# Second layer: mixer and both gates token-major, sums of weights from a column of ones, result transposed, norm factor behind the products

## Chip, cores and metric

The kernel runs on one core of a Trainium2 chip. The core has five engines that run side by side, each through its own list of instructions in a fixed order: TensorE (PE, matrix products; PEld is its loading of weights), VectorE (DVE), ScalarE (ACT), GpSimd (POOL) and SyncE (SP, which issues nearly all transfers here). They wait for each other by semaphores. The metric is the device time of one execution in microseconds, lower is better.

## What is computed

A trunk of two layers on 256 tokens of width 2048, in float32. The first layer (HGRN2 and RG-LRU) is not touched. The second is an mLSTM with two gates, then an output projection, a gated per-layer embedding and the final norm. Cut to the part that matters:

```python
hn = rmsnorm(h, o_norm[j])
u = hn @ o_w_in[j]                      # q,k (2048), v, og, z (2048 each), 2 x 8 gates
qk = jax.nn.silu(causal_conv(qk, c_conv_w[j], c_conv_b[j]))
li = ig + c_b_i[j]
lf = jax.nn.log_sigmoid(fg + c_b_f[j])
# mlstm, 8 heads of 128 (q, k) and 256 (v):
sc = jnp.einsum('bhtd,bhsd->bhts', qc, kc) * wts
num = g_inter * (qc @ c_st) + jnp.einsum('bhts,bhse->bhte', sc, vc)
den = g_inter * (qc @ n_st) + jnp.sum(sc, axis=-1)
hout = num / jnp.maximum(jnp.abs(den), jnp.exp(-m_t))[..., None]
# behind it:
yc = head_rmsnorm(hout, c_norm[j]) * jax.nn.sigmoid(og) * jax.nn.silu(z)
h = h + yc @ o_w_out[j]
pl = rmsnorm(p[i] @ ple_w[i], ple_norm[i])
h = h + jax.nn.sigmoid(h @ ple_gate_w[i]) * pl
```

The kernel computes the mLSTM over all 256 tokens at once, without the chunks.

## The kernel before, in words

**Precision.** Each large product is made of three: a float32 operand is split into a high and a low part (`whi`, `wlo` of the weights, both halves of `ahl` for activations), and high x high, high x low and low x high are summed. `load_weights` (L112) brings 128x2048 weights as two halves `raw`, ACT casts the high part (L123) and DVE subtracts (L124). There are five buffers for `raw`, four each for `whi` and `wlo`.

**Two forms of projection.** Feature-major (`block`, L147, through `project`, L182): 128 output features on the partitions, 256 tokens in the columns. 16 products of 512 columns (L154, high weights on both parts of the activations), then 16 of 256 columns (L160, low weights on the high part); `merge` (L177) adds the two halves of the PSUM bank by ACT (L179) and DVE (L180). Token-major (`project_tok`, L189): 128 tokens on the partitions, 512 features in the columns, two banks for the two halves of the tokens; the weights come in four quarters (`kq`), and each quarter has 12 products for each half (L204 to L206). The pool `pm` has three PSUM banks for both.

**Side work.** What is not a projection runs in generators, the lanes ("mix", "norm", "pl"). `pump` (L75) takes each lane one step further, in the middle of each block or quarter, so that its PE instructions lie between a block's products; `drain` runs a lane to its end. From this the framework makes one list per engine ahead of time, by priority, where a tile waits for a free buffer of its tag. The casts of weights have a raised priority.

**The second layer.** `finish_norm` (L471) makes the norm factors of the tokens (`norm["rt"]` with tokens on partitions, `norm["rs"]` with tokens in columns) and the normed activations `act` by `normed` (L300). `acth` is the same without the factor, only with the gain. v is projected token-major from `acth`, and the factor is applied as its result leaves PSUM (L781). The 16 gate columns (L802), q and k (`qk_proj`, L759), `oog` (eight pairs, L935) and `oz` (eight pairs, `gate_split`, L318) are feature-major products on `act`. The 12 buffers of the tag `ahl` hold `acth`, `act`, the embedding's input and the results `y` of the z gate.

**The mixer.** `gate_stats` (L813) makes the decays, their running maximum and `enm`, the Exp that bounds the denominator. `mix(j)` (L852) takes two heads in four steps: the maxima spread over the partitions and the weights' Exp; scores (L874, L875) and weighting; then, into feature-major banks, the sums of weights (L887, L888) and the value products (L892, L893), whose squares are summed by the next call (`head_sums`, L845). `mix_norm` (L903) turns denominators and sums of squares into one factor per head and token, spreads it by PE (L919) and multiplies `nums`. Then come the tanh gates, the splits of `y`, the embedding product `ple` (L339) and `finish_layer` (L382), whose first block reads all eight pairs of `y`.

## Time and profile before

| | |
|---|---|
| median of 3 runs | 1126.47 us (1126.02 to 1127.44) |
| the profiled execution | 1128.03 us |
| its span | 1126.3 us |
| mean granted clock of TensorE | 0.993 |
| share of PE in the chain that ended last | 90% |
| L154, L160: share of that chain | 48%, 25% |
| HBM read, written | 195.17 MB, 2.10 MB |

A profile is one execution. Busy time of an engine is the sum of stretches in which it had an instruction; times are in us from the start of the span unless marked ns. In a list of groups a row reads: line, engine, operation, output<-inputs, shapes and count, then busy time and mean ns of one, then the idle time of the engine before them and what ended it. In a list in order of time a row reads: start, length, engine, line, operation, count, and in brackets the idle time before it. In the chain the length is only the part that the next step waited for. In a table of stages each engine has its busy time and, in parentheses, the number of instructions; PEclk is the granted clock of TensorE. A plain float32 product is recorded as two matrix instructions.

### The profile page before, as it was taken

The page shows a single profiled execution, that of the slowest core. Times are in us where ns is not written, and L with a number is a line of the kernel's source. Part 1 is how long each engine was busy: PE and PEld are TensorE (multiplying, and loading weights), DVE is VectorE, ACT ScalarE, POOL GpSimd, SP SyncE. Part 2 cuts the span into 40 slices and gives each one's busy share as a digit, 9 for nine tenths or more (in the row PEclk, how much of TensorE's full clock was granted, in tenths as well). Part 3 has the DMA queues.
Part 4 walks back from the last instruction along what each step waited for, and adds up shares of the span by engine and source line. Part 5 has one row for each costly group of instructions (what it writes and reads, how often), then busy time and mean ns, then how long its engine had stood idle before and what let it go on. Part 6 is the DMA issues. An engine that isn't in the chain of part 4 may idle for free.

```text
span 1126.3 us, 16657 instructions
## 1 busy us (share of the span) xinstructions
PE 1102.8 (98%) x6344; PEld 958.6 (85%) x6344; DVE 806.6 (72%) x1192; ACT 593.2 (53%) x814; POOL 106.4 (9%) x78
## 2 busy tenths in 40 slices
PE   7999999999999999999999999999999989999996
PEld 6778898888888888888888888888888888888886
DVE  6998776798867656787745876659566568856774
ACT  6575435666645435555545655544455464435553
POOL 2144000000000000111000011110000013500110
PEclk9999999999999999999999999999999989999998
DMA  8655545443566555565555544444565555555542
GB/s 315 205 181 187 167 138 166 149 148 132 170 204 201 192 187 187 187 190 187 190 188 174 183 139 139 150 148 159 192 201 187 188 169 163 192 187 188 189 149 75
DMA packets 55377, 198.36 MB, mean 176 GB/s; under 512 B 6145, under 2 KB 6401, under 8 KB 55297
## 3 DMA queue, kind: packets, MB, share of 16 engines
q1 hardware_dynamic: 54720, 195.20, 52.4%
q0 software_dynamic: 576, 2.10, 0.6%
q8 instruction: 50, 0.82, 0.3%
q14 instruction: 31, 0.25, 0.1%
HBM read 195.17 MB, written 2.10 MB: 175 GB/s over the span
## 4 chain that ended last, share of the span: by engine, by line
PE 90%; DVE 2%; ACT 1%; issue 0%; POOL 0%; ACTq 0%; DVEq 0%; POOLq 0%
PE mm L154 48%; PE mm L160 25%; PE mm L204 2%; PE mm L206 2%; PE mm L205 2%; PE mx L589 2%; PE mx L892 1%; DVE wlo L124 1%; PE mx L687 1%; PE mm L171 1%; PE mm L143 0%; PE mm L144 0%; PE tr L959 0%; PE mm L145 0%; PE mx L277 0%
## 5 line engine op out<-in xcount | busy, mean ns | idle before, releaser
L124 DVE TENSOR_TENSOR wlo<-raw,whi 128x1024 fp32r<-128x1024 f32 (+1 forms) x361 | 456.7, 1300 | 204.1 <-issue 79.8
L154 PE MATMUL mm<-ahl,whi 128*128 128x512 f32 x2416 | 578.3, 391 | 2.3 <-DVE ahl L139 2.3
L123 ACT CAST whi<-raw 128x1024 fp32r<-128x1024 f32 (+1 forms) x361 | 376.4, 1046 | 293.2 <-PE mm L154 225.4
L154 PEld LDWEIGHTS mm<-ahl,whi 128*128 128x128 f32 x2416 | 443.4, 188 | 91.1 <-DVE ahl L139 4.4
L160 PE MATMUL mm<-ahl,wlo 128*128 128x256 f32 x2416 | 318.6, 285 | 0.0
L160 PEld LDWEIGHTS mm<-ahl,wlo 128*128 128x128 f32 x2416 | 307.3, 191 | 11.3 <-issue 1.3
L179 ACT COPY sm<-mm 128x256 f32<-128x256 f32 x119 | 44.0, 370 | 97.8 <-PE mm L160 97.6
L204 PE MATMUL mm<-whi,ahl 128*128 128x512 f32 x192 | 75.5, 393 | 0.1
L206 PE MATMUL mm<-whi,ahl 128*128 128x512 f32 x192 | 74.9, 391 | 0.1
L205 PE MATMUL mm<-wlo,ahl 128*128 128x512 f32 x192 | 74.9, 390 | 0.1
L298 POOL TENSOR_TENSOR acc<-acc,sq 128x512 f32<-128x512 f32 x17 | 27.6, 1621 | 298.7 <-ACT sq L297 223.8
L180 DVE TENSOR_TENSOR mg<-mm,sm 128x256 f32<-128x256 f32 x119 | 49.4, 416 | 0.1
L206 PEld LDWEIGHTS mm<-whi,ahl 128*128 128x128 f32 x192 | 36.0, 188 | 8.5 <-DVE ahl L139 1.0
L204 PEld LDWEIGHTS mm<-whi,ahl 128*128 128x128 f32 x192 | 36.1, 188 | 8.0 <-ACT ahl L138 0.5
L205 PEld LDWEIGHTS mm<-wlo,ahl 128*128 128x128 f32 x192 | 36.1, 188 | 7.8 <-DVE wlo L124 0.5
L298 POOL TENSOR_TENSOR placc<-placc,sq 128x512 f32<-128x512 f32 x14 | 22.7, 1624 | 203.1 <-ACT sq L297 177.7
L378 POOL TENSOR_TENSOR pl<-pl,plrs 128x512 f32<-128x512 f32 x16 | 30.0, 1908 | 33.5 <-ACT plrs L289 33.5
L143 PE MATMUL mm<-ahl,whi 128*128 128x256 f32 x64 | 21.1, 330 | 10.2 <-ACT whi L123 7.1
L769 DVE SCALAR_TENSOR_TENSOR qk<-mg,prm,qk 128x255 f32<-128x255 f32 (+2 forms) x48 | 22.2, 478 | 11.6 <-ACT qk L766 11.0
L138 ACT CAST ahl<-hn 128x512 fp32r<-128x512 f32 x32 | 19.4, 616 | 15.9 <-DVE hn L305 9.9
L745 POOL DMA_DIRECT2D hq<-in_xT_dram x4 | 2.3, 578 | 236.7 <-PE mx L641 179.2
L143 PEld LDWEIGHTS mm<-ahl,whi 128*128 128x128 f32 x64 | 14.8, 231 | 10.7 <-ACT whi L123 7.4
(249 smaller groups left out, 799.1 us busy)
## 6 DMA issues: line engine op xcount, KB each, us to landing
raw<-in_ew_dram SPq DMA_DIRECT2D x80, 512.0 KB, 4.5
raw<-in_g_dram SPq DMA_DIRECT2D x64, 512.0 KB, 4.5
raw<-in_eo_dram SPq DMA_DIRECT2D x32, 512.0 KB, 4.8
raw<-in_ov_dram SPq DMA_DIRECT2D x32, 512.0 KB, 4.2
raw<-in_oqk_dram SPq DMA_DIRECT2D x32, 512.0 KB, 4.3
raw<-in_oog_dram SPq DMA_DIRECT2D x32, 512.0 KB, 4.2
raw<-in_oz_dram SPq DMA_DIRECT2D x32, 512.0 KB, 4.4
raw<-in_oo_dram SPq DMA_DIRECT2D x32, 512.0 KB, 4.2
```

The lines of the kernel that those rows point to most:

```text
L123: last["act"] = s.copy(h, r).ins
L124: last["dve"] = v.tensor_tensor(out=l, in0=r, in1=h.bitcast(F32), op=ALU.subtract).ins
L143: te.matmul(o, whi, x[0][:, k], start=first, stop=False)
L154: last["pe"] = te.matmul(ps, parts[k // 8][0][:, c:c + P], act[k // 2][2][:, (k % 2) * 512:(k % 2 + 1) * 512], start=(k == 0), stop=False).ins
L160: last["pe"] = te.matmul(ps[:, T:2 * T], parts[k // 8][1][:, c:c + P], act[k // 2][0][:, k % 2], start=False, stop=(k == KT - 1)).ins
L179: s.copy(small, ps[:, T:2 * T])
L180: v.tensor_tensor(out=dst, in0=ps[:, 0:T], in1=small, op=ALU.add)
L204: te.matmul(ps[hf], xh, wh, start=(k == 0), stop=False)
L205: te.matmul(ps[hf], xh, wl, start=False, stop=False)
L206: last["pe"] = te.matmul(ps[hf], xl, wh, start=False, stop=(k == KT - 1)).ins
L298: eng.tensor_tensor(out=acc, in0=acc, in1=sq, op=ALU.add)
L378: gp.tensor_tensor(out=x3, in0=x3, in1=rs.unsqueeze(1).to_broadcast([P, 2, T]), op=ALU.mult)
```

## The change

v, `oog` and `oz` are now all token-major, from `acth`; `act` and its eight splits are gone. The norm factor of q, k and of the gate columns is multiplied in behind the product (`rs` of `project`; `gate_stats`), that of the two gates is the scale of their tanh and a part of `fac`. Each head's v has a 257th column of ones, so that one product gives numerators and the sum of weights; numerators lie with the tokens on the partitions, and sums of squares come with ACT's Square. `mix_norm` works on 16 columns, one per head and half of the tokens, and needs `enm` turned to that form, which two more small products in `gate_stats` do (L845 of the new kernel). A new lane "fm" turns each z result back by eight transposes (`feature_major`, L926) and splits it (L934, L935). The diff, cut (the removed bodies stand in the listing above):

```diff
-    def project(w, pair, act, which=(0, 1)):
+    def project(w, pair, act, which=(0, 1), rs=None):
...
             merge(m[:, j * T:(j + 1) * T], block(w[2 * pair + j], act))
+        if rs is not None:
+            m3 = m.rearrange("p (j t) -> p j t", t=T)
+            v.tensor_tensor(out=m3, in0=m3, in1=rs.unsqueeze(1).to_broadcast([P, 2, T]), op=ALU.mult)
...
         norm["rs"] = free_copy(norm["rt"], "hrs")
         yield
-        yield from normed(hq, norm["rs"], g, act)
+        if act is not None:
+            yield from normed(hq, norm["rs"], g, act)
...
-    act = []
     norm.clear()
-    start("norm", finish_norm(accs, hq, "on", act, 1))
+    start("norm", finish_norm(accs, hq, "on", None, 1))
...
-            ps = project(a["oqk"], j, act)
-            d = m1.tile([P, 512], F32, name="qk", tag="qk", bufs=10)
+            ps = project(a["oqk"], j, acth, rs=norm["rs"])
+            d = m1.tile([P, 512], F32, name="qk", tag="qk", bufs=8)
...
+        VW = 257
         vts = []
         for j in range(4):
             psv = project_tok(a["ov"], j, acth)
-            vt = m1.tile([P, 2, 512], F32, name="vt", tag="vt", bufs=4)
+
+            vt = m1.tile([P, 2, 2, VW], F32, name="vt", tag="vt", bufs=6)
+            gp.memset(vt[:, :, :, 256:VW], 1.0)
             for hf in range(2):
-                s.activation(vt[:, hf, :], psv[hf], AF.Copy, scale=norm["rt"][:, hf:hf + 1])
+                s.activation(vt[:, hf, :, 0:256], psv[hf].rearrange("p (i e) -> p i e", i=2), AF.Copy,
+                             scale=norm["rt"][:, hf:hf + 1])
             vts.append(vt)
         drain("norm")
+        rth = m1.tile([P, 2], F32, name="rth", bufs=1)
+        v.tensor_scalar(rth, norm["rt"], 0.5, None, op0=ALU.mult)
...
-                for i, x in enumerate(act[k // 2][0:2]):
+                for i, x in enumerate(acth[k // 2][0:2]):
...
-            s.activation(li, ps[0:8, 0:T], AF.Identity, bias=cbi)
-            s.activation(xf, ps[32:40, 0:T], AF.Identity)
-            v.scalar_tensor_tensor(xf, xf, cbf, ps[96:104, 0:T], op0=ALU.add, op1=ALU.add)
-            v.tensor_tensor(out=li, in0=li, in1=ps[64:72, 0:T], op=ALU.add)
+            for x, c, b in ((li, 0, cbi), (xf, 32, cbf)):
+                s.copy(x, ps[c:c + 8, 0:T])
+                v.tensor_tensor(out=x, in0=x, in1=ps[64 + c:72 + c, 0:T], op=ALU.add)
+                v.tensor_tensor(out=x, in0=x, in1=norm["rs"][0:8], op=ALU.mult)
+                v.tensor_scalar(x, x, b, None, op0=ALU.add)
...
-            for hf in range(2):
-                te.matmul(px_[:, hf * 8:hf * 8 + 8], av[:, hf * P:(hf + 1) * P], ident[0:8, 0:8],
-                          start=True, stop=True)
-            v.tensor_copy(aT, px_[:, 0:16])
+            for c, x in ((0, av), (16, enm)):
+                for hf in range(2):
+                    o = c + hf * 8
+                    te.matmul(px_[:, o:o + 8], x[:, hf * P:(hf + 1) * P], ident[0:8, 0:8], start=True, stop=True)
+            v.tensor_copy(aT, px_[:, 0:32])
...
-        def head_sums(j):
-            for i in range(2):
-                hd = 2 * j + i
-                te.matmul(acc8[1], sel8[:, hd, :], sqs8[hd][:, 0:T], start=(hd == 0), stop=(hd == 7))
...
+        den, ss, fac = (m1.tile([P, 16], F32, name=n, bufs=1) for n in ("den", "ss", "fac"))
...
-            sums = m1.tile([P, 2, P], F32, name="sums", tag="sums", bufs=1)
-            gp.tensor_tensor(out=sums, in0=scw[:, :, P:T], in1=scw[:, :, T:384], op=ALU.add)
...
             vt = vts[j]
+            nm = m1.tile([P, 2, 512], F32, name="num", tag="vt", bufs=6)
             for i in range(2):
+                pool, tag = ((px, "mx"), (pst, "st"))[i]
+                for hf in range(2):
+                    c = hf * 8 + 2 * j + i
+                    ps = pool.tile([P, 512], F32, name="nu", tag=tag)[:, 0:VW]
+                    te.matmul(ps, scw[:, i, hf * P:(hf + 1) * P], vt[:, 0, i], start=True, stop=(hf == 0))
+                    if hf:
+                        te.matmul(ps, scw[:, i, T:384], vt[:, 1, i], start=False, stop=True)
+                    o = nm[:, hf, i * 256:(i + 1) * 256]
+                    s.copy(o, ps[:, 0:256])
+                    v.tensor_copy(den[:, c:c + 1], ps[:, 256:VW])
+                    sq = tp.tile([P, 512], F32, name="sq", tag="sq")[:, 0:256]
+                    s.activation(sq, ps[:, 0:256], AF.Square, accum_out=ss[:, c:c + 1])
+            nums[j] = nm
...
+        def mix_norm():
+            t, r, yh = (m1.tile([P, 16], F32, name=n, bufs=1) for n in ("nwt", "nwr", "nwy"))
+            s.activation(den, den, AF.Abs)
+            v.tensor_tensor(out=den, in0=den, in1=aT[:, 16:32], op=ALU.max)
+            v.tensor_scalar(den, den, 1e21, EPS ** 0.5, op0=ALU.min, op1=ALU.mult)
+            v.tensor_tensor(out=den, in0=den, in1=den, op=ALU.mult)
+            v.scalar_tensor_tensor(den, ss, 1.0 / 256, den, op0=ALU.mult, op1=ALU.add)
+            newton(den, t, r, yh)
+            for hf in range(2):
+                c = slice(hf * 8, hf * 8 + 8)
+                v.tensor_scalar(fac[:, c], r[:, c], norm["rt"][:, hf:hf + 1], 0.25, op0=ALU.mult, op1=ALU.mult)
+            yield
+        y = []
+        def feature_major(j, u):
+            yield
+            yield
+            banks = []
+            for b in range(2):
                 ps = px.tile([P, 512], F32, name="mx", tag="mx")
+                for k in range(2):
+                    c = (2 * b + k) * P
+                    for hf in range(2):
+                        o = k * T + hf * P
+                        te.transpose(ps[:, o:o + P], u[:, hf, c:c + P], ident)
+                banks.append(ps)
+            yield
+            for b, ps in enumerate(banks):
+                hi, lo, both = act_pair()
+                for k in range(2):
+                    g = pc("cn", 4 * j + 2 * b + k)
+                    x = ps[:, k * T:(k + 1) * T]
+                    s.activation(hi[:, k], x, AF.Copy, scale=g)
+                    v.scalar_tensor_tensor(lo[:, k], x, g, hi[:, k].bitcast(F32), op0=ALU.mult, op1=ALU.subtract)
+                y.append((hi, lo, both))
...
-        for j in range(8):
-            ps = project(a["oog"], j, act)
-            th = m1.tile([P, 512], F32, name="tho", tag="vt", bufs=4)
-            s.activation(th, ps, AF.Tanh, scale=0.5)
+        for j in range(4):
+            ps = project_tok(a["oog"], j, acth)
+            th = m1.tile([P, 2, 512], F32, name="tho", tag="vt", bufs=6)
+            for hf in range(2):
+                s.activation(th[:, hf], ps[hf], AF.Tanh, scale=rth[:, hf:hf + 1])
             held.append((j, th))
             if j == 3:
                 drain("mix")
-            if j >= 3:
-                for jj, t in held:
-                    v.scalar_tensor_tensor(nums[jj], t, 1.0, nums[jj], op0=ALU.add, op1=ALU.mult)
-                held = []
+            for jj, th in [x for x in held if x[0] in nums]:
+                v.scalar_tensor_tensor(nums[jj], th, 1.0, nums[jj], op0=ALU.add, op1=ALU.mult)
+            held = [x for x in held if x[0] not in nums]
         pact = load_p(1)
-        y = []
-        for j in range(8):
-            y.append(gate_split(a["oz"], j, lambda: nums[j], False))
+        for j in range(4):
+            ps = project_tok(a["oz"], j, acth)
+            u = m1.tile([P, 2, 512], F32, name="u", tag="vt", bufs=6)
+            for hf in range(2):
+                s.activation(u[:, hf], ps[hf], AF.Tanh, scale=rth[:, hf:hf + 1])
+                v.scalar_tensor_tensor(u[:, hf], u[:, hf], 1.0, ps[hf], op0=ALU.add, op1=ALU.mult)
+                for i in range(2):
+                    c = hf * 8 + 2 * j + i
+                    e = slice(i * 256, (i + 1) * 256)
+                    v.scalar_tensor_tensor(u[:, hf, e], u[:, hf, e], fac[:, c:c + 1], nums[j][:, hf, e],
+                                           op0=ALU.mult, op1=ALU.mult)
+            start("fm", feature_major(j, u))
 
         pls = ple(1, pact, m1, "qk")
+        drain("fm")
...
-        "oog": _fm(ow[:, 4096:6144]),
-        "oz": _fm(ow[:, 6144:8192]),
+        "oog": _tm(ow[:, 4096:6144]),
+        "oz": _tm(ow[:, 6144:8192]),
```

The places in the engines' lists. A number behind a tile's name tells its instances apart, and brackets hold the engines and queues that an instruction waits for. First PE, where `mix` of the first two heads makes its value products, between the two halves of a q block. Before (the second head's six rows follow in the same form):

```order
L154 MATMUL mm_6192<-ahl_5402,whi_6200 128x512 x2
L887 MATMUL st_6221<-scw_6162,cst_80 8x128 [waits DVE_49]
L888 MATMUL st_6221<-sums_6171,cst_80 8x128 [waits Pool_49]
L892 MATMUL mx_6225<-scw_6162,vt_5220 128x256 [waits PE_49]
L893 MATMUL mx_6225<-scw_6162,vt_5220 128x128
```

After, both heads:

```order
L154 MATMUL mm_6158<-ahl_5034,whi_6166 128x512 x2
L887 MATMUL nu_6188<-vt_5218,scw_6130 128x257 [waits DVE_49]
L887 MATMUL nu_6194<-vt_5218,scw_6130 128x257 [waits PE_49]
L889 MATMUL nu_6194<-vt_5218,scw_6130 128x257
L887 MATMUL nu_6201<-vt_5218,scw_6130 128x257 [waits DVE_49]
L887 MATMUL nu_6207<-vt_5218,scw_6130 128x257
L889 MATMUL nu_6207<-vt_5218,scw_6130 128x257
```

Twelve products have become six, in the same place. Second ACT, during the first q blocks, where the gate statistics end. `sm` is the copy of a merge, `Bc` the tile of `enm`. Before:

```order
L823 ACTIVATE ab_5767<-ab_5767 8x256 [waits DVE_49]
L179 COPY sm_5835<-mm_5772 128x256 [waits PE_49]
L123 CAST whi_5953<-raw_5952 128x1024 [waits DMAHW5_49,PE_49]
L766 ACTIVATE qk_5886<-mg_5771,prm_79 128x256 [waits DVE_49]
L123 CAST whi_5959<-raw_5958 128x1024 [waits DMAHW6_49,PE_49]
L829 ACT_TABLE_LOAD
L829 ACTIVATE Bc_5768<-Bc_5768 8x256 [waits DVE_49]
L179 COPY sm_5883<-mm_5838 128x256 [waits PE_49]
L123 CAST whi_6014<-raw_6013 128x1024 [waits DMAHW7_49,PE_49]
```

After:

```order
L831 ACTIVATE ab_5723<-ab_5723 8x256 [waits DVE_49]
L123 CAST whi_5919<-raw_5918 128x1024 [waits DMAHW5_49,PE_49]
L123 CAST whi_5925<-raw_5924 128x1024 [waits DMAHW6_49,PE_49]
L179 COPY sm_5846<-mm_5801 128x256 [waits PE_49]
L123 CAST whi_5981<-raw_5980 128x1024 [waits DMAHW7_49,PE_49]
L837 ACT_TABLE_LOAD
L837 ACTIVATE Bc_5724<-Bc_5724 8x256 [waits DVE_49]
L767 ACTIVATE qk_5850<-mg_5730,prm_79 128x256 [waits DVE_49]
```

The Exp of `enm` has moved behind the second merge's copy and behind the cast of the fourth block's first weights. Third ACT again, around the end of the z projection and `ple` (`pl` is the copy that empties a bank of `ple`, `placc` and `sq` are its squares). Before, from `ple`'s first copy on:

```order
L356 COPY pl_8572<-mm_8573 128x512 [waits PE_49]
L322 ACTIVATE th_8346<-mg_8249 128x512 [waits DVE_49]
L322 ACTIVATE th_8450<-mg_8353 128x512 [waits DVE_49]
L123 CAST whi_8707<-raw_8706 128x1024 [waits DMAHW4_49,PE_49]
L327 CAST ahl_8248<-th_8346 128x2x256 [waits DVE_49]
L123 CAST whi_8713<-raw_8712 128x1024 [waits DMAHW5_49,PE_49]
L322 ACTIVATE th_8554<-mg_8457 128x512 [waits DVE_49]
L294 ACTIVATE placc_8734<-pl_8572 128x512
L327 CAST ahl_8352<-th_8450 128x2x256 [waits DVE_49]
L356 COPY pl_8602<-mm_8603 128x512
L327 CAST ahl_8456<-th_8554 128x2x256 [waits DVE_49]
```

After, from `ple`'s last copy on ACT:

```order
L359 COPY pl_8251<-mm_8252 128x512 [waits PE_49]
L123 CAST whi_8368<-raw_8367 128x1024 [waits DMAHW7_49,PE_49]
L934 ACTIVATE ahl_8291<-mx_8281,prm_79 128x256 [waits PE_49]
L934 ACTIVATE ahl_8296<-mx_8286,prm_79 128x256 [waits PE_49]
L300 ACTIVATE sq_8389<-pl_8221 128x512 [waits Pool_49]
L300 ACTIVATE sq_8392<-pl_8236 128x512 [waits DVE_49,Pool_49]
L934 ACTIVATE ahl_8291<-mx_8281,prm_79 128x256 [waits DVE_49]
L123 CAST whi_8424<-raw_8423 128x1024 [waits DMAHW0_49,PE_49]
L934 ACTIVATE ahl_8296<-mx_8286,prm_79 128x256 [waits DVE_49]
```

The tanh and the casts of `y` (L322, L327) that stood among `ple`'s copies are gone from there; the scaled copies of the last two pairs (L934) stand behind `ple`, with two squares and a cast between them.

51 lines of the change are left out of this document (3 added, 48 removed).

## Prediction

> **What bounds the kernel now.** I read the head of the page first, then a table of stages, then the order of events on TensorE (PE) in the second layer.
>
> ```profile
> span 1126.3 us, 16657 instructions
> PE 1102.8 (98%) x6344; PEld 958.6 (85%) x6344; DVE 806.6 (72%) x1192; ACT 593.2 (53%) x814; POOL 106.4 (9%) x78
> ```
>
> PE is busy for 98% of the span. An engine that is this full sets the time, so an edit counts by the PE time that it adds or takes, and by the new waits that it gives PE.
>
> ```profile
> core 0: us, PE busy (x) PEld busy (x) DVE busy (x) ACT busy (x) POOL busy (x), PEclk, DMA share, GB/s
> 545.00:611.00 66.00, 66.00 (x295) 54.70 (x294) 37.40 (x47) 31.97 (x42) 1.91 (x2) 1.00 0.54 179
> 611.00:740.00 129.00, 129.00 (x744) 109.36 (x743) 92.56 (x139) 77.63 (x119) 11.47 (x9) 1.00 0.48 156
> 825.00:914.00 89.00, 89.00 (x514) 78.65 (x513) 53.07 (x64) 45.34 (x60) 0.00 (x0) 1.00 0.58 190
> 914.00:932.00 18.00, 14.94 (x101) 14.61 (x101) 14.92 (x21) 12.16 (x20) 4.13 (x3) 0.81 0.37 122
> ```
>
> The stages are the v projection (545 to 611), q and k with most of the mixer (611 to 740), the z gate (825 to 914) and the second embedding product, `ple` (914 to 932). PE has no gap in the first three. Only `ple` has one, and only there is the granted clock below 1.00. DVE is at 72% of the q and k stage, ACT at 60%: there is room beside PE.
>
> **Gates.** Before, each of the 32 blocks of `oog` and `oz` is 16 products of 512 columns and 16 of 256.
>
> ```profile
> 780.51 3.65 PE mm L154 x16
> ...
> 908.55 3.65 PE mm L154 x16
> ```
>
> In this list of PE's chain 23 blocks lie between those starts: 128.04 / 23 = 5.567 us each, 22.27 for the four that make 512 output columns. The token-major form is the one that v uses now (`project_tok`), 96 products of 512 columns a call.
>
> ```profile
> L204 PE MATMUL mm<-whi,ahl x100: 389/389/585, 542.4 to 609.9; 128*128 128x512 f32 x100
> ```
>
> L204 is the first of three products of a step. 99 steps take 67.5 us, 0.682 each, and 32 steps make a call: 21.82 us. So a call saves 0.45 us and eight calls **3.6 us**. The merges (L179, L180) go too, but they stood beside a full PE and count nothing.
>
> The Trainium skill ("TensorE: Matmul & The Clock Gate", section "Back-to-back issue gap") gives N/2.4 + 2.5 ns a product; by it a call would save an estimated 0.08 us, eight calls 0.6, and the sum would be 3 us smaller. The blocks above take about 10 ns more per product than that, so here the trace decides.
>
> **Mixer.** What is put between a block's two halves is read as the time from L154's start to L160's start, less the undisturbed 3.65.
>
> ```profile
> 643.82 3.82 PE L154 MATMUL mm<-ahl,whi 128*128 128x512 f32 x16
> 647.47 2.08 PE L160 MATMUL mm<-ahl,wlo 128*128 128x256 f32 x16
> ...
> 656.26 3.82 PE L154 MATMUL mm<-ahl,whi 128*128 128x512 f32 x16
> ...
> 660.54 0.70 PE L892 MATMUL mx<-scw,vt 128*128 128x256 f32 x2
> 661.08 0.38 PE L893 MATMUL mx<-scw,vt 128*128 128x128 f32 x2
> 661.30 0.60 PE L892 MATMUL mx<-scw,vt 128*128 128x256 f32 x2
> 661.74 0.38 PE L893 MATMUL mx<-scw,vt 128*128 128x128 f32 x2
> ...
> 663.91 2.16 PE L160 MATMUL mm<-ahl,wlo 128*128 128x256 f32 x16
> 754.32 3.81 PE L154 MATMUL mm<-ahl,whi 128*128 128x512 f32 x16
> 759.03 2.17 PE L160 MATMUL mm<-ahl,wlo 128*128 128x256 f32 x16
> 766.60 3.81 PE L154 MATMUL mm<-ahl,whi 128*128 128x512 f32 x16
> 771.46 2.18 PE L160 MATMUL mm<-ahl,wlo 128*128 128x256 f32 x16
> ```
>
> The value products with the sums of weights cost 7.65 - 3.65 = 4.00 us a call of `mix`. A plain float32 product of 256 columns takes 661.74 - 661.30 = 0.44 us, two records. After the change a call has six of 257 columns: 6 x 0.44 = 2.64, and 0.16 for the slower start of the group (the first took 0.54): 2.80. Four calls save **4.8 us**. A width of 257 is in no row. From below 0.44 bounds it, since it has more columns than 256; from above 0.88, if the odd column were paid as a second pass. I take 0.44, the nearest row.
>
> The sums of squares (`head_sums`) go: 4.71 - 3.65 = 1.06, four times, **4.2 us**. Two groups of eight spreads of the norm factor go: 4.86 - 3.65 = 1.21 each, **2.4 us**. In their place come column operations of DVE (16 copies of one column, one Newton chain on 16 columns) and ACT squares. At 72% and 60% these engines hide them under PE's blocks; without that cover they would show as a wait before the spreads, which stand a block (5.57 us) behind the products.
>
> **Transposes back.** Each of the four results needs eight transposes; the kernel's last stage has such ones now.
>
> ```profile
> 1110.92 2.78 PE L959 MATMUL tr<-cst,hq 128*128 128x128 f32 x24
> 1113.54 0.50 PE L238 MATMUL st<-ones,acc 128*128 128x1 f32 x4
> ```
>
> 24 take 2.62 us, 0.109 each; eight 0.87, with 0.1 for the start of a group 0.97, four groups **+3.9 us**. Their operands are ready some ten us earlier for the first three; the fourth stands behind `ple`, whose 11.5 us cover it.
>
> **The embedding product.** Here the change moves a stall away.
>
> ```profile
> 914.11 0.12 PE mm L143
> ...
> 922.93 0.58 PE mm L143
> ...
> 931.43 3.65 PE mm L154 x16
> 863.13 0.62 ACT L327 CAST ahl<-th 128x512 fp32r<-128x512 f32 x1
> ...
> 913.19 1.14 ACT L327 CAST ahl<-th 128x512 fp32r<-128x512 f32 x2
> ```
>
> 96 products of 0.12 us are 11.5 us, but the stage took 931.43 - 914.11 = 17.3. PE stood still until 922.93, and at clock 0.81 on the mean some of the rest was slow. The reason is in the last two rows: three of the eight splits of `y` (L327) ran during the z stage, and the other five came after its end, because the buffers of their results are those of `act`, which every block reads to the last. So ACT did splits and tanh ahead of the copies that free PSUM for `ple`. After the change `acth` is read in quarters, and the first quarter of the last call already frees buffers: six of eight splits are done before `ple`, and ACT's order there holds copies, casts and squares. I followed that order with ACT at 0.6 us for a copy or square and 1.05 for a cast, and no copy ends later than PE wants its bank. So the 5.8 us go: **-5.8 us**. What is late next is the last pair of splits, below.
>
> **New waits.** First the gate statistics. Their last operation, an Exp, is now read by PE (two more small products, L845, behind the third q block) and was not before.
>
> ```profile
> 624.89 1.28 ACT L829 ACT_TABLE_LOAD   x1
> 626.18 0.42 ACT L829 ACTIVATE Bc<-Bc 8x256 f32<-8x256 f32 x1
> ...
> 627.58 1.06 ACT L123 CAST whi<-raw 128x1024 fp32r<-128x1024 f32 x1 [0.72 <-PE mm L154]
> 629.28 0.61 PE L835 MATMUL mx<-cst,li 8*128 8x8 f32 x4
> 629.82 2.17 PE L160 MATMUL mm<-ahl,wlo 128*128 128x256 f32 x16
> ```
>
> In the new order of ACT a cast that waits for PE, the one at 627.58, stands ahead of the table load and the Exp. So the Exp ends at 627.58 + 1.05 + 1.28 + 0.42 = 630.3, while PE would reach those products 0.27 after 629.28: a stall of 0.8, with the semaphore **0.9 us**, and **0.4** for the two products (a pair costs 629.82 - 629.28 = 0.54 with its start). Behind them on PE stand L160 and the whole main stream. Bounds 0 and 2.3: none if the cast starts earlier, 2.3 if one more cast (1.05) and one merge copy (0.37) get ahead.
>
> Second the last two splits, whose transposes PE does right behind `ple`. PE then has 12 products before it needs the seventh pair, 14 before the second half: 0.87 + 13 x 0.228 = 3.8 us behind the end of `ple`. ACT has by its order one cast (1.05, released by `ple`'s last product), two scaled copies, two squares, then the scaled copy in question, and DVE one pass.
>
> ```profile
> L766 ACT ACTIVATE qk<-mg,prm 128x256 f32<-128x256 f32 x16 | 9.6, 597 | 6.0 <-DVE mg L180 6.0
> L179 ACT COPY sm<-mm 128x256 f32<-128x256 f32 x119 | 44.0, 370 | 97.8 <-PE mm L160 97.6
> L769 DVE SCALAR_TENSOR_TENSOR qk<-mg,prm,qk 128x255 f32<-128x255 f32 (+2 forms) x48 | 22.2, 478 | 11.6 <-ACT qk L766 11.0
> ```
>
> With 0.2 for a semaphore, 1.05, five ACT operations and 0.48 on DVE: 4.7 at 0.6 each, 3.6 at 0.37, 4.3 at 0.5. I take **0.5 us**; the ends are 0 and 0.9. It is the same place on which the stall of now stood, so 5.8 is the far end.
>
> **Edits with no cost.** The split of the normed activations (16 DVE passes, eight splits) leaves the v stage, where PE was full anyway: nothing. The factor on q and k adds eight DVE passes over 128x512.
>
> ```profile
> L773 DVE SCALAR_TENSOR_TENSOR qk<-th,qk 128x512 f32<-128x512 f32 x8 | 5.5, 682 | 0.0
> ```
>
> At 0.68 us they are 5.5 on 92.56 of 129 us, 76%, under PE's blocks. Four small memsets on GpSimd stand behind a fold that is done before v's results are.
>
> **Sum.** -3.6 - 4.8 - 4.2 - 2.4 + 3.9 - 5.8 + 0.9 + 0.4 + 0.5 = -15.1 us. Against the profiled span that is 1111.2; that execution took 1128.03, 1.7 more than its span, and would take 1112.9. The runs shown have the median 1126.47, 1.6 below it, and I forecast against that: **1111.3 us**.
>
> **Rivals.**
> 1. The stall at `ple` keeps its size (ACT's queue is static, and copies still stand behind casts that wait for PE). Then 5.8 are not gained: 1117.1. Against it: five gate splits with their tanh are out of that queue. Chance 0.14.
> 2. A width of 257 costs two passes: 24 products x 0.44 = 10.6 more, 1121.9. For it: no row has an odd width on PE, and the second head's columns start 257 elements on. Against: two records of 256 columns already run at the pace of their columns. Chance 0.09.
> 3. The token-major call gains nothing, if PE pays columns alone: both forms stream the same number of columns, 64 x 512 + 64 x 256 = 96 x 512. Without those 3.6 us it is 1114.9. Against: the measured pace of both forms. The rule quoted above points this way. Chance 0.07.
> 4. Slower: in the token-major form PE needs the low half of the weights with the second product of a quarter, not 3.65 us later, and in the z stage DVE has three passes more per result half between those subtractions, in order. If each of the 16 quarters of `oz` waited for one subtraction,
>
> ```profile
> L124 DVE TENSOR_TENSOR wlo<-raw,whi 128x1024 fp32r<-128x1024 f32 (+1 forms) x361 | 456.7, 1300 | 204.1 <-issue 79.8
> ```
>
> at 1.3 us, that is +20.8: 1132.1. It decides from 15.1 / 16 = 0.94 us a quarter on. Against it: v runs in the same form, with the split of the normed activations on the same engines, and PE is busy 66.00 of 66.00 us. Chance 0.06.
> 5. Rivals 1 and 2 together: 1127.7, no change that can be told. Chance 0.04.
>
> **Numbers.** The forecast has 0.60. A measurement tells 0.2% here, 2.25 us. Faster: 0.60 + 0.14 + 0.09 + 0.07 = 0.90; the same 0.04; slower 0.06. The range reaches down to 1108 (neither new wait, no start costs of groups: 1.4 + 0.6 + 0.4 less is 1108.9) and up to 1122, which takes in rivals 1 to 3 and the bound on the odd width; rivals 4 and 5 are left out.
>
> **What would show it.** Right: value products of 0.44 us; calls of `oog` and `oz` 21.8 us apart without inserted work; PE at the clock 1.00 through `ple`, which takes 11.5 us; a wait of PE for the Exp near the third q block, near 1 us. Wrong: PE waiting for low halves in the z stage, a wait above 2 us for the last pair of `y` with a lower clock behind it, or 257-column records of 0.4 us.

## The result, and the profile after

| | before | changed |
|---|---|---|
| median | 1126.5 us (1126.02 to 1127.44, 4 runs) | 1110.4 us (1110.02 to 1110.71, 4 runs) |
| ratio, 95% interval | | 0.985 (0.984 to 0.987) |
| the profiled execution, its span | 1128.03, 1126.3 us | 1110.02, 1108.3 us |

The changed kernel takes 16.1 us less, where 15.2 were forecast. The spans of the two profiles differ by 18.0. That difference needs a look of its own (below). First the head of the page of the changed kernel, then its table of stages, cut as before the change as far as the stages still exist.

```profile
span 1108.3 us, 15932 instructions
PE 1087.6 (98%) x6044; PEld 941.2 (85%) x6044; DVE 783.5 (71%) x1160; ACT 582.3 (53%) x814; POOL 91.4 (8%) x70
```

```profile
core 0: us, PE busy (x) PEld busy (x) DVE busy (x) ACT busy (x) POOL busy (x), PEclk, DMA share, GB/s
545.00:611.00 66.00, 66.00 (x298) 54.91 (x297) 28.28 (x28) 28.57 (x34) 1.91 (x2) 1.00 0.53 176
611.00:740.00 129.00, 128.48 (x711) 111.37 (x710) 99.98 (x165) 78.41 (x142) 0.00 (x0) 1.00 0.50 167
825.00:900.00 75.00, 75.00 (x345) 62.34 (x344) 47.76 (x59) 37.91 (x46) 0.00 (x0) 1.00 0.57 188
900.00:912.00 12.00, 12.00 (x101) 11.92 (x100) 10.09 (x12) 9.13 (x15) 3.43 (x3) 1.00 0.60 200
```

PE is as full as before (98%) and has 300 instructions fewer. The embedding product is now a stage like the others: PE busy 12.00 of 12.00 us at the clock 1.00, where before it had 14.94 of 18.00 at 0.81. The one new gap in these stages is the 0.52 us missing from the q and k stage. DVE went from 92.56 to 99.98 in that stage, 78%, and that gap of PE is put down to ACT in the list below.

Next, PE's list in order of time at four places of the changed kernel: a call of `mix` with its value products, the third q block with the new wait, two groups of transposes in the z gate, and the way into and out of the embedding product.

```profile
656.41 3.82 PE L154 MATMUL mm<-ahl,whi 128*128 128x512 f32 x16
660.06 1.03 PE L887 MATMUL nu<-vt,scw 128*128 128x257 f32 x4
660.93 0.60 PE L889 MATMUL nu<-vt,scw 128*128 128x257 f32 x2
661.36 1.03 PE L887 MATMUL nu<-vt,scw 128*128 128x257 f32 x4
662.23 0.60 PE L889 MATMUL nu<-vt,scw 128*128 128x257 f32 x2
662.47 2.27 PE L160 MATMUL mm<-ahl,wlo 128*128 128x256 f32 x16
664.57 0.63 PE L154 MATMUL mm<-ahl,whi 128*128 128x512 f32 x2
...
624.56 3.81 PE L154 MATMUL mm<-ahl,whi 128*128 128x512 f32 x16
628.31 0.61 PE L845 MATMUL mx<-cst,li 8*128 8x8 f32 x4
629.44 0.61 PE L845 MATMUL mx<-cst,Bc 8*128 8x8 f32 x4 [0.52 <-ACT Bc L837]
...
845.95 1.03 PE L926 MATMUL mx<-cst,u 128*128 128x128 f32 x8
...
847.52 0.39 PE L207 MATMUL mm<-whi,ahl 128*128 128x512 f32 x1
...
867.92 0.39 PE L207 MATMUL mm<-whi,ahl 128*128 128x512 f32 x1
...
868.60 1.04 PE L926 MATMUL mx<-cst,u 128*128 128x128 f32 x8
...
900.33 0.28 PE L143 MATMUL mm<-ahl,whi 128*128 128x256 f32 x1
911.85 1.03 PE L926 MATMUL mx<-cst,u 128*128 128x128 f32 x8
912.64 5.10 PE L154 MATMUL mm<-ahl,whi 128*128 128x512 f32 x20
917.58 2.08 PE L160 MATMUL mm<-ahl,wlo 128*128 128x256 f32 x16
```

The second column is the modelled end of the last product and overlaps what follows, so I read starts alone. One product of 257 columns takes 661.36 - 660.93 = 0.43 us, two take 660.93 - 660.06 = 0.87. The whole block with the value products in it, from its L154 to the next L154, takes 664.57 - 656.41 = 8.16, and 8.16 - 5.57 = 2.59 is their price. L207 is the first of the three products of a step. Between the two rows of L207 lie 30 steps without other work: 20.40 us, 0.680 each, so a call's 32 steps take 21.76. From one group of transposes to the next is one call of the z gate and eight transposes: 22.65, less the 21.76 of a call 0.89. The embedding product takes 911.85 - 900.33 = 11.52, which is 96 x 0.12.

The block of before that held the value products ended here, in the same list for the kernel before (its start, 656.26, stands in the prediction):

```profile
665.91 1.32 PE L154 MATMUL mm<-ahl,whi 128*128 128x512 f32 x5
```

665.91 - 656.26 = 9.65, less 5.57 is 4.08 us a call. To tell stages apart from what happens at the start of an execution, I cut every profile at the same four products of PE:

| us | before | before, second profile | changed | changed, second profile |
|---|---|---|---|---|
| start to the first q block | 614.40 | 613.44 | 613.43 | 613.85 |
| first q block to embedding product | 299.55 | 299.54 | 286.90 | 286.96 |
| embedding product, with transposes | 17.32 | 16.32 | 12.31 | 12.31 |
| from there to the last stage's first transposes | 179.65 | 179.64 | 180.27 | 180.29 |

The second row repeats within 0.1 us, so 12.6 us of the gain lie there. The embedding product and the start do not repeat in the kernel before. The second profiles come from the experiments.

### The profile page after: what moved, and what is told of

It reads as the page before. It is cut to its first block, busy times and chain, and to the rows that moved or that the text cites. A ratio compares the mean times of both kernels' runs of the same rounds, so it can differ in the third digit from the quotient of the medians.

```text
span 1108.3 us, 15932 instructions
## 1 busy us (share of the span) xinstructions
PE 1087.6 (98%) x6044; PEld 941.2 (85%) x6044; DVE 783.5 (71%) x1160; ACT 582.3 (53%) x814; POOL 91.4 (8%) x70
## 4 chain that ended last, share of the span: by engine, by line
PE 90%; DVE 2%; ACT 0%; issue 0%; POOL 0%; DVEq 0%; ACTq 0%; POOLq 0%
PE mm L154 38%; PE mm L160 21%; PE mm L207 8%; PE mm L208 8%; PE mm L209 8%; PE mx L591 2%; PE mx L689 1%; PE nu L887 1%; DVE wlo L124 1%; PE mm L171 1%; PE mm L145 0%; PE mm L144 0%; PE mm L143 0%; PE mm L809 0%; PE st L650 0%
## 5 line engine op out<-in xcount | busy, mean ns | idle before, releaser
L154 PE MATMUL mm<-ahl,whi 128*128 128x512 f32 x1904 | 456.6, 391 | 2.0 <-DVE ahl L139 2.0
L154 PEld LDWEIGHTS mm<-ahl,whi 128*128 128x128 f32 x1904 | 349.5, 188 | 72.9 <-DVE ahl L139 4.1
L160 PE MATMUL mm<-ahl,wlo 128*128 128x256 f32 x1904 | 253.4, 286 | 0.0
L160 PEld LDWEIGHTS mm<-ahl,wlo 128*128 128x128 f32 x1904 | 243.8, 192 | 8.5 <-issue 0.9
L207 PE MATMUL mm<-whi,ahl 128*128 128x512 f32 x448 | 175.9, 393 | 0.1
L209 PE MATMUL mm<-whi,ahl 128*128 128x512 f32 x448 | 174.5, 390 | 0.1
L208 PE MATMUL mm<-wlo,ahl 128*128 128x512 f32 x448 | 174.4, 389 | 0.0
L209 PEld LDWEIGHTS mm<-whi,ahl 128*128 128x128 f32 x448 | 84.1, 188 | 18.6 <-DVE ahl L139 1.0
L207 PEld LDWEIGHTS mm<-whi,ahl 128*128 128x128 f32 x448 | 84.1, 188 | 18.0 <-ACT ahl L138 0.5
L208 PEld LDWEIGHTS mm<-wlo,ahl 128*128 128x128 f32 x448 | 84.2, 188 | 17.4 <-DVE wlo L124 0.4
L179 ACT COPY sm<-mm 128x256 f32<-128x256 f32 x87 | 32.1, 370 | 75.5 <-PE mm L160 75.2
L180 DVE TENSOR_TENSOR mg<-mm,sm 128x256 f32<-128x256 f32 x87 | 36.1, 416 | 0.1
```

The costliest lines, as they stand in the source:

```text
L154: last["pe"] = te.matmul(ps, parts[k // 8][0][:, c:c + P], act[k // 2][2][:, (k % 2) * 512:(k % 2 + 1) * 512], start=(k == 0), stop=False).ins
L160: last["pe"] = te.matmul(ps[:, T:2 * T], parts[k // 8][1][:, c:c + P], act[k // 2][0][:, k % 2], start=False, stop=(k == KT - 1)).ins
L179: s.copy(small, ps[:, T:2 * T])
L180: v.tensor_tensor(out=dst, in0=ps[:, 0:T], in1=small, op=ALU.add)
L207: te.matmul(ps[hf], xh, wh, start=(k == 0), stop=False)
L208: te.matmul(ps[hf], xh, wl, start=False, stop=False)
```

## The experiments

### The changed kernel and the kernel before once more

The changed kernel was run beside experiments 2 to 4 as their mark.

> The changed kernel once more, as the mark for the three runs beside it. Both theories expect what it took before: 1110.4 us, a ratio to the kernel before of 0.985 (0.984 to 0.987).

Measured: 1109.98 us, ratio 0.985 (0.984 to 0.987). The kernel before got a second profile:

> The kernel before once more, for a second profile of it. From the first q block to the end the stages sum to 17.0 us between the two profiles shown, while the medians differ by 16.1, and the profiled execution of before took 1.5 us more than its median. If that is the start of the execution (the first weights' arrival), the stages of this profile agree with the first within 0.2 us (299.55 from the first q block to the embedding product, 17.32 for that product) and only the time of the first q block (614.40) differs. If the stall at the embedding product varies by itself, 17.32 differs by 0.5 or more.

Measured: 1125.99 us. Both of the causes that the expectation names are at work. The first q block starts 0.96 us earlier than in the first profile, and the embedding product is 1.0 us shorter. PE's first product behind the stall, in the first profile and then in the second:

```profile
922.93 0.58 PE L143 MATMUL mm<-ahl,whi 128*128 128x256 f32 x1 [3.06 <-ACT pl L356]
```

```profile
921.96 0.39 PE L143 MATMUL mm<-ahl,whi 128*128 128x256 f32 x1 [3.06 <-ACT pl L356]
```

The table of stages, cut finely, shows what differs, first for the first profile, then for the second one; the columns are those above.

```profile
920.00:922.00 2.00, 0.00 (x0) 0.00 (x0) 2.00 (x4) 2.00 (x4) 0.00 (x0) 0.95 0.39 119
922.00:924.00 2.00, 1.07 (x5) 1.07 (x6) 2.00 (x4) 0.88 (x2) 0.00 (x0) 0.50 0.63 190
924.00:926.00 2.00, 2.00 (x11) 2.00 (x11) 2.00 (x4) 1.69 (x3) 0.37 (x1) 0.50 0.59 221
926.00:928.00 2.00, 2.00 (x11) 2.00 (x10) 0.03 (x1) 0.88 (x3) 1.92 (x2) 0.50 0.00 0
928.00:930.00 2.00, 2.00 (x16) 2.00 (x16) 1.37 (x2) 1.29 (x2) 1.84 (x2) 0.84 0.00 0
```

```profile
919.00:921.00 2.00, 0.00 (x0) 0.00 (x0) 2.00 (x4) 2.00 (x4) 0.00 (x0) 1.00 0.40 117
921.00:923.00 2.00, 1.04 (x7) 1.04 (x8) 2.00 (x4) 0.91 (x2) 0.00 (x0) 0.88 0.62 199
923.00:925.00 2.00, 2.00 (x11) 2.00 (x11) 2.00 (x4) 1.66 (x3) 0.33 (x1) 0.50 0.60 217
925.00:927.00 2.00, 2.00 (x15) 2.00 (x15) 0.43 (x2) 0.88 (x3) 1.92 (x2) 0.76 0.00 0
```

PE stands still for the same 3.06 us in both (3.2, if the last product before it is counted as 0.12 us long like the others). What differs is the slow clock behind it. A clock of 0.95 over 2 us is 0.2 us at half clock, and so on: the first execution was at half clock for 0.2 + 6.0 + 0.64 = 6.8 us, from 1.1 us before PE went on to about 928.6, the second for 0.48 + 2.0 + 0.96 = 3.4 us, and only after the first products. The products take 0.21 us each there, not 0.12, and that costs 2.6 us in the first execution and 1.6 in the second. With the second profile the stages give 286.9 - 299.5, 12.3 - 16.3 and 180.3 - 179.6, together -16.0 us, against the measured -16.1. So the 18.0 between the first two spans hold 1.0 us of slow clock and 1.0 us of the start, which belong to that execution and not to the change.

### The buffers of the z gate's results, in the kernel before

```diff
-    def act_pair():
+    def act_pair(own=None, tag="ahl", **bufs):
-        x = ap.tile([P, 1024], F32R, name="ahl", tag="ahl")
+        x = (own or ap).tile([P, 1024], F32R, name="ahl", tag=tag, **bufs)
...
-            y.append(gate_split(a["oz"], j, lambda: nums[j], False))
+            own = () if j < 3 else (m1, "vt", 4) if j < 7 else (m1, "y7", 1)
+            y.append(gate_split(a["oz"], j, lambda: nums[j], False, own))
```

> The kernel before, with nothing changed but the buffers of the last five results of the z gate (y): they lie in the four buffers of v's results, which are free by then, and in one of their own, and no longer wait until the normed activations are read for the last time. Nothing of the computation changes. Theory A, of the prediction: the stall at the second embedding product comes from those buffers, and through them from the order of ACT. Then all eight splits but the last are done before the embedding product, PE has no wait there, the stage from its first product to the first product of the next projection takes 11.5 to 12.5 us in place of 17.3, and the time falls by 4.8 to 5.8 us, to about 1121. Rival B: the stall comes from the rest of ACT's and DVE's work there (copies behind casts that wait for PE) and has nothing to do with those buffers: 17 us stay, 1126.5. Rival C: the token-major form itself took the stall away in the changed kernel (fewer operations of ACT and DVE behind each product); then a part of it, 2 to 4 us, stays here.

Measured: 1121.44 us (1120.99 to 1121.64), ratio 0.9953 (0.9940 to 0.9965), 5.0 us less than before. Theory A. The chain that ended last in the kernel before, at the stall (start, length, what):

```profile
919.63 0.14 PE mm L144
919.77 0.02 issue
919.79 1.05 ACT whi L123
920.84 0.53 ACT th L322
921.37 0.52 ACT placc L294
921.89 0.51 ACT ahl L327
922.40 0.49 ACT pl L356
```

PE's next product waits for the last row, the copy that frees its PSUM bank, and ahead of that copy ACT has a cast, a tanh, a square and a split in a row. ACT's list in order of time in this experiment:

```profile
917.57 0.59 ACT L356 COPY pl<-mm 128x512 f32<-128x512 f32 x1 [0.47 <-PE mm L145]
918.05 0.62 ACT L327 CAST ahl<-th 128x512 fp32r<-128x512 f32 x1
918.93 1.05 ACT L123 CAST whi<-raw 128x1024 fp32r<-128x1024 f32 x1 [0.26 <-ACT ahl L327]
...
920.94 0.56 ACT L356 COPY pl<-mm 128x512 f32<-128x512 f32 x1
```

Here a copy goes out at 917.57 already, and the last split of `y` follows it at 918.05. PE has no wait left in the embedding product: from its first product at 913.05 to the next block's at 924.57 it takes 11.52 us, as in the changed kernel. So the buffers alone were the cause of that stall. Rival C would have left 2 to 4 us for the token-major form to take away; nothing is left. The changed kernel gets its buffers in another way, by reading `acth` in quarters, and its trace fits that: the scaled copies of the fourth pair of `y` (L934) start at 882.89, within the last z call, those of the fifth and sixth at 891.89, all ahead of the embedding product at 900.33. No run changed the order of reading alone.

### The norm factor behind the products, alone, in the kernel before

```diff
-        yield from normed(hq, norm["rs"], g, act)
+        if act is not None:
+            yield from normed(hq, norm["rs"], g, act)
...
-            ps = project(a["oqk"], j, act)
+            ps = project(a["oqk"], j, acth, rs=norm["rs"])
...
-            ps = project(a["oog"], j, act)
+            ps = project(a["oog"], j, acth, rs=norm["rs"])
...
-            y.append(gate_split(a["oz"], j, lambda: nums[j], False))
+            y.append(gate_split(a["oz"], j, lambda: nums[j], False, acth, norm["rs"]))
```

> The kernel before, with one part of the change alone: the norm factor of q, k, both gates and the 16 gate columns is multiplied in behind the products, which read the activations without it; the split of the normed activations is gone. All forms, the mixer and the gates stay feature-major. Nothing of the computation changes. Theory A: this part is worth nothing by itself, since its 16 DVE passes and eight splits lay beside a full PE and its new passes do too, and the buffers of y are held as long as before by the other activations: within 0.7 us of 1126.5, and the stall at the embedding product stays at 17 us. Rival B: the removed split was on the path, in the stage of v or at its start: 2 us or more less. Rival C: the 24 new DVE passes over 128x512 delay merges or low halves of weights: 1 us or more above.

Measured: 1126.37 us, ratio 0.9997 (0.9988 to 1.0006). The stage from the first q block to the embedding product takes 299.54 us, as before, and PE's list still holds the stall:

```profile
921.53 0.38 PE L143 MATMUL mm<-ahl,whi 128*128 128x256 f32 x1 [2.61 <-ACT pl L359]
```

Theory A: this part of the change is worth nothing alone. It is what lets the gates read `acth`. The stall did not stay quite as it was: it is 0.45 us shorter, with the slow clock behind it the embedding product takes 15.90 us, and the stretch from there to the last transposes takes 180.00, 0.36 more than in the second profile of before.

### The normed activations made again, unused, in the changed kernel

```diff
-    start("norm", finish_norm(accs, hq, "on", None, 1))
+    start("norm", finish_norm(accs, hq, "on", [], 1))
```

> The changed kernel with the normed activations made again, as before the change (16 DVE passes, eight splits on ACT and DVE), though nothing reads them now. The result does not change. Theory A, of the prediction: they lie beside a full PE and cost nothing, 1110.4 within 0.4. Rival B: they hold up the casts or low halves of v's and q's weights: a wait of PE between 545 and 660 us and 1 us or more above.

Measured: 1110.37 us, ratio 0.9853 (0.9835 to 0.9870), no difference. The v stage shows the dead work, DVE at 37.75 us in place of 28.28, beside a PE that stays full:

```profile
545.00:611.00 66.00, 66.00 (x297) 54.79 (x296) 37.75 (x47) 31.98 (x41) 1.91 (x2) 1.00 0.53 176
```

### Value products of 256 columns

```diff
+        NW = 256
...
-                    te.matmul(ps, scw[:, i, hf * P:(hf + 1) * P], vt[:, 0, i], start=True, stop=(hf == 0))
+                    te.matmul(ps[:, 0:NW], scw[:, i, hf * P:(hf + 1) * P], vt[:, 0, i, 0:NW], start=True, stop=(hf == 0))
...
-                    v.tensor_copy(den[:, c:c + 1], ps[:, 256:VW])
+                    v.tensor_copy(den[:, c:c + 1], ps[:, 255:256])
```

> The changed kernel with value products of 256 columns in place of 257; the column of ones is left out of them and the denominators are copied from the last value column, so they are not the sums of weights. Theory A: the product's price is its columns, and the 257th is free: 0.43 us a product as in the changed kernel, the same time, 1110.4 within 0.3. Rival B: the odd width costs something in the rows' starts or in the copies: the four groups of six products shrink by 0.1 us a product or more, 2.4 us less in all.

Measured: 1110.51 us, ratio 0.985 (0.984 to 0.987), and 286.86 us from the first q block to the embedding product, against 286.96 in the mark. The column of ones is free; the odd width costs nothing.

### The `oog` gate feature-major in the changed kernel

```diff
-            ps = project_tok(a["oog"], j, acth)
+            ps = [block(a["oog"][4 * j + b], acth) for b in range(4)]
```

> The changed kernel with the oog gate's products in the feature-major form (four blocks a call), their banks neither merged nor turned, so that the gate is not the reference's. Weights, columns and transfers stay the same in number. Theory A: the feature-major form costs 22.27 us a call where the token-major one costs 21.82, so four calls cost 1.8 us more, 1112.2. Rival B, PE pays columns alone: the same time as the changed kernel, 1110.4.

Measured: 1112.49 us (1111.87 to 1112.89), ratio 0.987 (0.986 to 0.989), 2.1 us more than the changed kernel at first and 2.5 more than the mark; its stage from the first q block to the embedding product takes 289.24 us, 2.3 more. In the chain of this kernel twelve starts lie between

```profile
746.96 3.65 PE mm L154 x16
...
813.76 0.23 PE mm L207
```

66.80 / 12 = 5.567 a block, to the last digit what the prediction read in the kernel before. Four calls of 22.27 in place of 21.76 are 2.0. Of the rest, 0.3 is a pause in PE's list: the third block of the gate, with the scores in it, takes 7.18 us from 731.35 to the next block's start at 738.53, where a block with scores takes 6.88 elsewhere, and the profile names nothing that the weight load in front of 738.53 waited for. The mixer's groups themselves cost the same here and between quarters (the scores 1.31 us in both). PE does not pay columns alone. A 256-column product takes 1.91 / 16 = 0.1194 in that chain, and two of them 0.011 more than one of 512 (3.65 / 16 = 0.228); a feature-major call has 64 of the short ones where the token-major one has 32 long ones, of 0.680 / 3 = 0.227 each.

### Three attempts on the new waits

The first moves the products that read `enm` to `mix_norm`:

```diff
-            for c, x in ((0, av), (16, enm)):
...
+            for hf in range(2):
+                te.matmul(px_[:, hf * 8:hf * 8 + 8], av[:, hf * P:(hf + 1) * P], ident[0:8, 0:8],
+                          start=True, stop=True)
...
+            pe_ = px.tile([P, 512], F32, name="mx", tag="mx")
+            for hf in range(2):
+                te.matmul(pe_[:, hf * 8:hf * 8 + 8], enm[:, hf * P:(hf + 1) * P], ident[0:8, 0:8],
+                          start=True, stop=True)
...
```

> The changed kernel with the two small products that turn enm (L845) moved out of the gate statistics into mix_norm, some 30 us later, when the Exp is long done. Nothing of the computation changes. Theory A, the wait for the Exp is a real stall of PE: the piece between the third q block's halves falls from 1.66 us to the 0.54 that it took before the change, and the pair shows again in mix_norm at 0.3 to 0.5, so 0.6 to 0.8 us less, 1109.7, and no wait of PE at ACT's Bc. Rival B, what waits for the gate statistics takes the wait over (the maxima spread at the start of the first call of mix, or the reading of the denominators in mix_norm): the same time as the changed kernel, 1110.4, and a new row of waiting at one of those places.

Measured: 1108.76 us (1108.47 to 1109.87), ratio 0.985 (0.983 to 0.986). Its PE in order of time:

```profile
627.57 0.61 PE L843 MATMUL mx<-cst,li 8*128 8x8 f32 x4
628.11 1.10 PE L160 MATMUL mm<-ahl,wlo 128*128 128x256 f32 x7
...
746.26 0.61 PE L903 MATMUL mx<-cst,Bc 8*128 8x8 f32 x4
```

The piece in the third q block is 0.54 long again and the wait is gone, so it was PE's own. The pair now costs about 0.75 us in `mix_norm`, and the stage is 286.60, 0.36 less than the mark. The median is lower by another 0.9 us, and by the profile that is not the edit's: the first q block already starts 1.16 us earlier than in the mark, ahead of anything that was edited, and PE's waits for its first weights sum to 5.7 us where they are 7.2 in the mark. The two other runs with the same edit do not show it.

The second raises the priority of the splits, and a further run combines both:

```diff
-                for k in range(2):
...
+                with tc.high_priority(offset=400):
+                    for k in range(2):
...
```

> The changed kernel with the splits of the transposed results (L934, L935) raised in priority over the squares of the embedding product. Nothing of the computation changes. Theory A, the last low half of y is what PE waits for in the first block of the last layer's projection: its 20 products of the high weights, 4.94 us from start to the next group where 20 x 0.228 = 4.56 would do, take 4.6, and the time falls by 0.3 to 0.4 us to 1110.0. Rival B, those 0.38 us are no wait for y: 4.9 us stay, and the time is 1110.4.

> The two edits before together. Nothing of the computation changes. Theory A (both waits are PE's own): 0.9 to 1.2 us less than the changed kernel, 1109.3. Rival B (the waits move elsewhere): 1110.4, as the changed kernel.

Measured: 1110.00 us for the second and 1109.98 for both, ratios 0.985 (0.984 to 0.987, both). The priority did not do what I wanted: ACT still has two squares of the embedding's norm ahead of the third scaled copy, and the wait of PE's weight load for the low half stays. From the list of its waits:

```profile
PEld mm L154 <- DVE ahl L936: 0.4, 1, 0.4
```

So that run tests nothing about the wait. In the run with both edits the stage to the embedding product is 286.57, again 0.39 below the mark, while its time is the mark's. The third attempt moves the last transposes, with the splits behind them, between the two halves of the embedding product:

```diff
-        pls = ple(1, pact, m1, "qk")
-        drain("fm")
+        pls = ple(1, pact, m1, "qk", between=lambda: drain("fm"))
```

> The changed kernel with the last transposes and the splits behind them put between the two halves of the embedding product, about 5.8 us earlier. Nothing of the computation changes. Theory A, the 0.38 us in the first block of the last projection are PE's wait for the last low half of y: that half is made 4 us before PE needs it, the 20 products take 4.6 us in place of 4.94, and the time is 0.4 less, 1110.0; the transposes cost the same at the other place. Rival B: the four scaled copies (0.47 each) now stand ahead of ACT's copies that free PSUM for the embedding product, and PE waits there: 0.5 to 2 us in the embedding product, which takes 12.9 or more with the transposes, and the time is above 1110.5.

Measured: 1110.47 us, ratio 0.986 (0.984 to 0.987). Theory A is right about the place: the first block takes 5.57 again, and the weight load no longer waits for `ahl`. The transposes stage is 0.08 longer, no rival B. And yet the stretch behind it takes 180.32, as in the mark (180.29). The waits of the weight loads between 911 and 945 us, first in the mark, then here:

```profile
PEld st L264 <- DVE dg L261: 0.5, 1, 0.5
PEld mm L154 <- DVE ahl L935: 0.4, 1, 0.4
```

```profile
PEld st L264 <- DVE dg L261: 1.0, 1, 1.0
```

The 0.4 us came back 24 us later: the norm of the embedding (squares on ACT, sums on GpSimd, `dg` on DVE) ends when it ended before, and PE now reaches it earlier and waits longer. That wait was the next one in the row, which neither theory had named. With the moved `enm` pair as well:

> The same, with the two small products for enm in mix_norm as well. Nothing of the computation changes. By the stages measured for the one edit (0.37 less between the first q block and the embedding product) and the theory of the other (0.4): 0.75 us less than the changed kernel, 1109.5. If the last splits cost what rival B of the run before says: 1110.5 or more.

Measured: 1110.78 us, ratio 0.9861 (0.9845 to 0.9876): no gain. Stage by stage it has the 0.37 of the `enm` pair (286.59) and lost it to a start that was 0.6 us later than the mark's. None of these versions is shown to beat the changed kernel; the one gain that the stages bear out is that of the `enm` pair, 0.4 us, below what the times can tell.

## Why the prediction was right, point by point

The forecast was 1111.3 us and the time 1110.4. By terms, in us; "measured" comes from the starts on PE in the profiles:

| step of the prediction | forecast | measured |
|---|---|---|
| gates token-major | -3.6 | -4.1 (blocks of 5.567, calls of 21.76) |
| value products and sums of weights | -4.8 | -5.9 (4.08 to 2.59 a call) |
| sums of squares | -4.2 | -4.0 |
| spreads of the factor | -2.4 | -2.6 |
| transposes back | +3.9 | +3.5 (three of 0.89, the last 0.79) |
| wait for the Exp, two more products | +1.3 | +1.1 (the block takes 7.42, from 624.56 to 631.98, where it took 6.29 before) |
| stall at the embedding product | -5.8 | -5.8 and -4.8 in two profiles, -5.0 timed |
| last splits | +0.5 | +0.4, with 0.2 behind it +0.6 |
| sum | -15.1 | -16.2 with the stall of 4.8 (stages: -16.0) |

The 0.2 us between the last sum and the stages are in part the steps right behind a group of the mixer in the `oog` calls, which take 0.69 in place of 0.680.

That the forecast came within 0.9 us is in part luck: two gains that were put too small (value products and gates) and one that was put too large (the stall) nearly cancel, as told below.

**Gates.** The mechanism was right and the size 0.5 us short: the step of 0.682 was a mean over v's stage, and the steps without other work take 0.680. The experiment with `oog` shows the sign and the 2.0 us of its half. By the rule of the Trainium skill ("TensorE: Matmul & The Clock Gate", section "Back-to-back issue gap") that the prediction weighed and left (rival 3) that run should have cost an estimated 0.3 us; it cost 2.1 to 2.5. The section gives that rule for an isolated product and says itself that it does not hold for a stream in which every product loads its weights, as these do.

**Value products.** The mechanism was right and the size was 1.1 us off, the largest miss in the list. The new price was put at 2.80 with 0.16 for a slow start of the group; the start is not slow, 6 x 0.43 = 2.6. The old price was read to the start of L160, 4.00, while 0.08 of the last product shows only inside L160's group; from block to block it is 4.08. Reading from one L154 to the next avoids this. Rival 2 is refuted twice, by the rows of 0.43 us and by the run with 256 columns.

**Transposes.** The same assumed start of a group, 0.1, is nearly absent: 0.89 against 0.97 forecast, where eight transposes at 0.109 are 0.87.

**Sums of squares and spreads.** Three of the four sums shared a block with another group and cost 0.95 us each, the last alone cost 1.15; a group of spreads cost 1.3 and not 1.21, for the same reason as the value products: the time is read from block to block.

**Embedding product.** The cause was right, and the run with other buffers shows it without the rest of the change. The size has two parts. The wait of 3.2 us was the same in both profiles of the kernel before; the slow clock behind it cost 2.6 us in the execution that I read and 1.6 in the other. I took 5.8 off the median, though part of what set that profiled execution above the median was this very stall: 1.0 us was counted twice. By luck it nearly made up for the 1.1 of the value products.

**Waits that came new.** Both stand where they were forecast. The Exp holds PE for 0.52 us, not 0.9. The Exp itself came when forecast, 15.95 us behind the start of the first q block (forecast 630.3 - 614.4 = 15.9), but the products ahead of it take PE 0.61 us, not 0.27. No row shows the 0.1 and 0.2 us that the forecast allowed for a semaphore: the Exp ends at 629.38 and PE goes on at 629.44. For the last splits, the sum at 0.5 us an operation is 4.2, not 4.3, which gives the 0.4 that was measured. The last low half of `y` holds PE for 0.4, and the experiment showed that this is not worth removing, since PE then waits longer for the embedding's norm.

**Edits with no cost.** Shown from both sides: the norm factor behind the products changed nothing in the kernel before, and the old split of the activations put back changed nothing in the new one.

**Rival 4**, low halves late in the z gate: PE is busy for 75.00 of 75.00 us there, and two groups of transposes are 22.65 apart, one call and the eight transposes. It did not occur.

## What to carry to other kernels

When a stall disappears, ask which buffer held it: five buffers alone brought 5 of the 16 us here, without any new form of product. A gap that ends in a lowered clock costs more than the gap, and here its second part differed between executions, so take its size from two profiles and not from the one that lies above the median. Price inserted work from one block's start to the next block's start, and before removing a small wait look for the next one on the same path.

## What the runs showed of the hardware

The price of the slow clock after a gap is not fixed. With the same gap of 3.2 us between the same two products, PE was back at 0.12 us a product 5.7 us after the gap's end in one execution and 4.0 in the other. In the run with the norm factor behind the products a gap of 2.8 us was enough: the granted clock was 0.65, 0.50, 0.50 and 0.64 in the four microseconds from 922 on, 3.4 us at half clock. So the three stretches at half clock lasted 6.8, 3.4 and 3.4 us; three executions show this, and no run was made to test it. The Trainium skill ("TensorE: Matmul & The Clock Gate", Part 1 on the clock gate) says that the gate watches a free-running window of about 3.4 us, so that the count of slow products at the start of a kernel differs between its runs. These profiles agree with the variation, and their slow stretches are as long as one or two such windows, while their gaps of 3.2 and 2.8 us are shorter than one.

The start of the program differs from one execution to the next: the first q block, behind the same products of PE, began between 612.69 and 614.45 us in the profiles, and in two of them PE's waits for its first weights summed to 5.7 and 7.2 us. For differences below 1 us, stages cut at the same product of PE told more here than the medians.

A plain float32 product of 257 columns costs what one of 256 does, 0.43 us, in the changed kernel and in the run with 256 columns.
